# Grouped instance normalisation on one core: normalising on VectorE alone with half the instructions, and two early loads on the ScalarE queue

## Chip, core and metric

The kernel runs on one core of a Trainium2 chip. The metric is the device time of one execution in microseconds (us). The span that a profile shows is about 1.7 us shorter than that time. Where two kernels are compared by a ratio, it is the mean time of one kernel's fast runs over the mean of the other's of the same rounds, so it is not quite the ratio of the medians that are quoted.

## The reference

Shortened:

```python
def setup_inputs():
    B, G, C_per_g, H, W = 4, 8, 16, 256, 256       # x: 512 channels of 65536 float32, gamma: 128
    ...

def reference(x, gamma):
    mu = x.mean(axis=(3, 4), keepdims=True)
    var = ((x - mu) ** 2).mean(axis=(3, 4), keepdims=True)
    x_norm = (x - mu) / np.sqrt(var + 1e-5)
    return (x_norm * gamma[None, :, :, None, None]).astype(np.float32)
```

134.22 MB come in and 134.22 MB go out; every element is read once and written once.

## The kernel before

The input is cut into 32 units of 16 channels. A unit is a tile of 128 partitions by 8192 columns, 4 MB: a channel lies on 8 partitions. The kernel keeps six tiles in the on-chip memory. A unit is loaded, its sums and sums of squares are taken per partition, a small matmul averages them over the 8 partitions of a channel (its result, the tile `ps`, lies in the memory that the program calls PSUM), a row of tiny operations makes a scale and a shift, VectorE normalises 5376 columns and ScalarE the other 2816, and the unit is stored. Loads go out on the SyncE queue, stores on the ScalarE queue. Load u+6 waits until store u has freed its tile (26 waits of the SyncE queue for stores in the trace, 502.8 us in all).

```python
    for u in range(6):
        load(u)                                     # all on nc.sync
    g_row = singles.tile([1, G * C], F32, name="g_row")
    nc.scalar.dma_start(out=g_row[:], in_=gv[None, :])
    # ... constants, the averaging matrix, gamma brought to one value per partition ...

    def coefficients(u):
        # ... sums: one reduce_sum over 8192 columns; sqs: two Square activations of 4096 columns ...
        mv = stats_pool.tile([P, 2], F32, name="mv")
        nc.vector.reduce_sum(out=mv[:, 0:1], in_=sums[:], axis=AX.X)
        nc.vector.reduce_sum(out=mv[:, 1:2], in_=sqs[:], axis=AX.X)
        # ... matmul with avg into ps ...
        nc.vector.tensor_copy(out=cm[:], in_=ps[:])
        # ... nmean = -mean; var = E[x^2] - mean^2; std (ScalarE Sqrt); rstd; scale = rstd * gamma ...
        nc.vector.tensor_mul(out=shift[:], in0=nmean[:], in1=scale[:])
        return scale, shift
    # ...
    for u in range(U):
        scale, shift = coefficients(u)
        t = tiles.pop(u)
        # ... (store_spans is empty)
            norm_vector(t, 0, DV, scale, shift)     # DV = 5376
            norm_scalar(t, DV, F, scale, shift)
            nc.scalar.dma_start(out=ov[u], in_=t[:])
        if u + 6 < U:
            load(u + 6)
```

Of the kernel before, what the change touches and what calls it, by code (L numbers as in the profile page):

```python
# [6 lines left out]

F32 = mybir.dt.float32
BF16 = mybir.dt.bfloat16
ALU = mybir.AluOpType  # L10
ACTF = mybir.ActivationFunctionType
AX = mybir.AxisListType


@with_exitstack
def kernel(
    ctx: ExitStack,
    tc: tile.TileContext,
    x: bass.AP,
    gamma: bass.AP,  # L20
    out: bass.AP,
):
    nc = tc.nc
    B, G, C, H, W = x.shape
    P = nc.NUM_PARTITIONS
    HW = H * W
    n_ch = B * G * C
    S = 8
    K = P // S
    F = HW // S  # L30
    U = n_ch // K
    NG = (G * C) // K
    SQ = 4096
    DV = 5376
    assert HW % S == 0 and (G * C) % K == 0 and F % SQ == 0

    xv = x.rearrange("b g c h w -> (b g c h w)").rearrange("(u p f) -> u p f", p=P, f=F)
    ov = out.rearrange("b g c h w -> (b g c h w)").rearrange("(u p f) -> u p f", p=P, f=F)
    gv = gamma.rearrange("g c -> (g c)")

    data = ctx.enter_context(tc.tile_pool(name="data", bufs=6))
    singles = ctx.enter_context(tc.tile_pool(name="singles", bufs=1))
    stats_pool = ctx.enter_context(tc.tile_pool(name="stats", bufs=2))
    psum = ctx.enter_context(tc.tile_pool(name="psum", bufs=2, space=bass.MemoryType.PSUM))
    ctx.enter_context(tc.manual_schedule())

    def spans(widths):
        edges = [0]
        for w in widths:
            edges.append(edges[-1] + w)  # L50
        assert edges[-1] == F
        return list(zip(edges[:-1], edges[1:]))

    load_spans, store_spans = {}, {}
    whole = spans([F])

    tiles = {}

    def load(u):
        t = data.tile([P, F], F32, name="xt")  # L60
        for a, b in load_spans.get(u, whole):
            nc.sync.dma_start(out=t[:, a:b], in_=xv[u, :, a:b])
        tiles[u] = t

    for u in range(6):
        load(u)


    g_row = singles.tile([1, G * C], F32, name="g_row")
    nc.scalar.dma_start(out=g_row[:], in_=gv[None, :])  # L70
    eps_t = singles.tile([P, 1], F32, name="eps_t")
    nc.vector.memset(eps_t[:], 1e-5)
    avg = singles.tile([P, K, S], F32, name="avg")
    nc.gpsimd.memset(avg[:], 1.0 / HW)
    nc.gpsimd.affine_select(
        out=avg[:], in_=avg[:], pattern=[[-S, K], [0, S]], compare_op=ALU.is_ge,
        fill=0.0, base=0, channel_multiplier=1,
    )
    nc.gpsimd.affine_select(
        out=avg[:], in_=avg[:], pattern=[[S, K], [0, S]], compare_op=ALU.is_ge,  # L80
        fill=0.0, base=S - 1, channel_multiplier=-1,
    )
    one = singles.tile([1, 1], F32, name="one")
    nc.vector.memset(one[:], 1.0)
    g_rep = singles.tile([1, NG, K, S], F32, name="g_rep")
    nc.vector.tensor_copy(  # L86
        out=g_rep[:],
        in_=g_row[:].rearrange("o (n k) -> o n k", n=NG).unsqueeze(3).to_broadcast([1, NG, K, S]),
    )
    g_ps = psum.tile([P, NG], F32, name="g_ps", bufs=1)  # L90
    for n in range(NG):
        nc.tensor.matmul(  # L92
            out=g_ps[:, n : n + 1],
            lhsT=g_rep[:, n].rearrange("o k s -> o (k s)"),
            rhs=one[:],
            start=True, stop=True,
        )
    g_col = singles.tile([P, NG], F32, name="g_col")
    nc.vector.tensor_copy(out=g_col[:], in_=g_ps[:])  # L99

    junk = singles.tile([P, SQ], BF16, name="junk")

    def coefficients(u):
        t = tiles[u]
        sums = stats_pool.tile([P, len(load_spans.get(u, whole))], F32, name="sums")
        sqs = stats_pool.tile([P, F // SQ], F32, name="sqs")
        n = 0
        for j, (a, b) in enumerate(load_spans.get(u, whole)):
            nc.vector.reduce_sum(out=sums[:, j : j + 1], in_=t[:, a:b], axis=AX.X)  # L109
            for c in range(a, b, SQ):  # L110
                nc.scalar.activation(  # L111
                    out=junk[:], in_=t[:, c : c + SQ], func=ACTF.Square,
                    accum_out=sqs[:, n : n + 1],
                )
                n += 1
        mv = stats_pool.tile([P, 2], F32, name="mv")
        nc.vector.reduce_sum(out=mv[:, 0:1], in_=sums[:], axis=AX.X)  # L117
        nc.vector.reduce_sum(out=mv[:, 1:2], in_=sqs[:], axis=AX.X)  # L118
        ps = psum.tile([P, 2], F32, name="ps")
        nc.tensor.matmul(  # L120
            out=ps[:], lhsT=avg[:].rearrange("p k s -> p (k s)"), rhs=mv[:],
            start=True, stop=True,
        )
        cm = stats_pool.tile([P, 2], F32, name="cm")
        nc.vector.tensor_copy(out=cm[:], in_=ps[:])  # L125
        nmean = stats_pool.tile([P, 1], F32, name="nmean")
        nc.vector.tensor_scalar(  # L127
            out=nmean[:], in0=cm[:, 0:1], scalar1=-1.0, scalar2=None, op0=ALU.mult,
        )
        var = stats_pool.tile([P, 1], F32, name="var")  # L130
        nc.vector.scalar_tensor_tensor(  # L131
            out=var[:], in0=cm[:, 0:1], scalar=nmean[:], in1=cm[:, 1:2],
            op0=ALU.mult, op1=ALU.add,
        )
        std = stats_pool.tile([P, 1], F32, name="std")
        nc.scalar.activation(out=std[:], in_=var[:], func=ACTF.Sqrt, bias=eps_t[:], scale=1.0)  # L136
        rstd = stats_pool.tile([P, 1], F32, name="rstd")
        nc.vector.reciprocal(out=rstd[:], in_=std[:])  # L138
        scale = stats_pool.tile([P, 1], F32, name="scale")
        g = u % NG  # L140
        nc.vector.tensor_mul(out=scale[:], in0=rstd[:], in1=g_col[:, g : g + 1])  # L141
        shift = stats_pool.tile([P, 1], F32, name="shift")
        nc.vector.tensor_mul(out=shift[:], in0=nmean[:], in1=scale[:])  # L143
        return scale, shift

    def norm_vector(t, a, b, scale, shift):
        nc.vector.tensor_scalar(  # L147
            out=t[:, a:b], in0=t[:, a:b], scalar1=scale[:], scalar2=shift[:],
            op0=ALU.mult, op1=ALU.add,
        )  # L150

    def norm_scalar(t, a, b, scale, shift):
        nc.scalar.activation(  # L153
            out=t[:, a:b], in_=t[:, a:b], func=ACTF.Identity, bias=shift[:], scale=scale[:],
        )

    for u in range(U):
        scale, shift = coefficients(u)
        t = tiles.pop(u)
        if u in store_spans:  # L160
            for j, (a, b) in enumerate(store_spans[u]):
                (norm_scalar if j == 1 else norm_vector)(t, a, b, scale, shift)
            for a, b in store_spans[u]:
                nc.scalar.dma_start(out=ov[u, :, a:b], in_=t[:, a:b])
        else:
            norm_vector(t, 0, DV, scale, shift)
            norm_scalar(t, DV, F, scale, shift)
            nc.scalar.dma_start(out=ov[u], in_=t[:])
        if u + 6 < U:
            load(u + 6)  # L170


# [28 lines left out]
```

## Time and profile before

| | before |
|---|---|
| time, median of 3 runs | 628.93 us (628.9 to 629.06) |
| span of the profile | 627.1 us |
| instructions | 937, of them 324 on VectorE and 194 on ScalarE |
| bytes moved | 268.4 MB, mean 428 GB/s |
| VectorE / ScalarE busy | 66% / 54% |

The first lines come from the page of the kernel before: the span, busy time by engine (PE is TensorE and PEld its weight loads, DVE is VectorE, ACT is ScalarE, POOL is GpSimd), two rows of 40 slices of 15.7 us each (busy tenths of the 16 DMA engines, and GB/s), and the DMA queues. Queue q1 carries the loads, q10 the stores and the gamma row; q14 is the one whose kind the page gives as `instruction`.

```profile
span 627.1 us, 937 instructions
...
PE 22.3 (4%) x80; PEld 19.5 (3%) x80; DVE 416.5 (66%) x324; ACT 336.9 (54%) x194; POOL 1.2 (0%) x7
...
DMA  8999999999999999999999999999999999999997
GB/s 368 435 403 433 435 435 435 433 435 435 435 433 435 435 435 431 433 428 433 435 427 435 431 435 433 433 433 435 435 433 435 435 435 435 433 433 435 435 433 314
...
q1 hardware_dynamic: 4608, 134.22, 49.9%
q10 hardware_dynamic: 4610, 134.22, 49.6%
q14 instruction: 6, 0.05, 0.0%
```

The DMA engines are busy nine tenths or more in every slice but the first and the last, at 427 to 435 GB/s in all of these but the third (403). At 433 GB/s, the rate of the trace from 50 to 620 us, the bytes alone need 620 us, so the kernel stands within 1.5% of the time that its traffic takes at that rate. No compute engine is near its limit: the busiest, VectorE, works 66% of the span.

The next lines are the costliest groups of instructions (busy us, mean ns of one, then the engine's idle time before them and what ended it).

```profile
L109 DVE TENSOR_REDUCE sums<-xt 128x1 f32<-128x8192 f32 x32 | 277.9, 8686 | 150.4 <-DMA xt<-in_x_dram 150.4
L111 ACT ACTIVATE junk<-xt 128x4096 bf16<-128x4096 f32 x64 | 231.5, 3617 | 166.8 <-DMA xt<-in_x_dram 163.5
L147 DVE TENSOR_SCALAR xt<-xt,scale,shift 128x5376 f32<-128x5376 f32 x32 | 98.5, 3079 | 1.2
L153 ACT ACTIVATE xt<-xt,shift,scale 128x2816 f32<-128x2816 f32 x32 | 87.5, 2734 | 22.0 <-DVE shift L143 22.0
```

VectorE waits 150 us in all for loads. A unit's chain takes 14.2 us (from a reduction's start to the end of the normalise), and a unit lands every 19.35 us.

The last lines are of the view by windows: for stretches near the end, their length, each engine's busy time, the granted clock, the mean share of the 16 DMA engines that was busy, and GB/s.

```profile
core 0: us, PE busy (x) PEld busy (x) DVE busy (x) ACT busy (x) POOL busy (x), PEclk, DMA share, GB/s
...
620.00:622.00 2.00, 0.00 (x0) 0.00 (x0) 0.00 (x0) 0.00 (x0) 0.00 (x0) 1.00 0.68 295
622.00:624.00 2.00, 0.00 (x0) 0.00 (x0) 0.00 (x0) 0.00 (x0) 0.00 (x0) 1.00 0.65 279
624.00:626.00 2.00, 0.00 (x0) 0.00 (x0) 0.00 (x0) 0.00 (x0) 0.00 (x0) 1.00 0.08 33
626.00:628.00 2.00, 0.00 (x0) 0.00 (x0) 0.00 (x0) 0.00 (x0) 0.00 (x0) 1.00 0.00 0
```

A share of 0.06 would be one DMA engine of sixteen at work all the time; single windows read too high or too low where packets cross their edges (1.22 from 618 to 620 us, 0.68 from 620 to 622). Between 622 and 626 us the rate falls to 279 and then 33 GB/s.

The trace also has a record of every DMA packet. Each transfer of 4 MB gives every DMA engine eight packets of 32 KB, 1.213 us each (96% of them in this trace), and then a packet of 4 bytes, which I take for its report that it is done: each transfer has 128 of the large packets and 16 of these, and each of these starts within 0.013 us of the end of a data packet. So for the last store one can read when each engine finished (us after the first data packet, which comes 1.8 us into the span; lists of packets are on this clock, windows on the span's):

```
before, the 16 engines at the end of the last store:
621.53 621.54 621.55 621.58 621.59 621.60 621.62 621.68 621.69 621.71 621.71 621.72 621.76 622.56 623.45 623.93
```

Thirteen engines finish within 0.23 us, three come after, the last 2.24 us behind the median. The kernel ends with the last one: in all eleven profiles the span ends 1.3 to 1.6 us after it.

### The profile page before, as it was taken

How to read it: one execution, taken by the hardware profiler on the slowest of the kernel's cores; microseconds unless marked ns; L12 is line 12 of the kernel's file. 1: busy time of each engine (PE TensorE's matmuls, PEld its weight loads, DVE VectorE, ACT ScalarE, POOL GpSimd, SP SyncE). 2: the span in 40 equal slices, each digit the busy share in tenths (PEclk: the TensorE clock that was granted, in tenths of full speed). 3: DMA queues.
4: the chain of work that ended last, by engine and by line, in shares of the span. 5: the costliest groups of instructions: out<-in, count | busy, mean ns of one | idle time of the engine just before them, and what ended most of it. 6: DMA issues, size and time to landing. Idle time of an engine off the chain costs nothing.

```text
span 627.1 us, 937 instructions
## 1 busy us (share of the span) xinstructions
PE 22.3 (4%) x80; PEld 19.5 (3%) x80; DVE 416.5 (66%) x324; ACT 336.9 (54%) x194; POOL 1.2 (0%) x7
## 2 busy tenths in 40 slices
PE   2000000000000000000000000000000000000000
PEld 2000000000000000000000000000000000000000
DVE  2999657766577665686656866558665577655770
ACT  2877536555456464464634646446554455544560
POOL 0000000000000000000000000000000000000000
DMA  8999999999999999999999999999999999999997
GB/s 368 435 403 433 435 435 435 433 435 435 435 433 435 435 435 431 433 428 433 435 427 435 431 435 433 433 433 435 435 433 435 435 435 435 433 433 435 435 433 314
DMA packets 9224, 268.49 MB, mean 428 GB/s; under 512 B 1025, under 2 KB 1026, under 8 KB 1026
## 3 DMA queue, kind: packets, MB, share of 16 engines
q1 hardware_dynamic: 4608, 134.22, 49.9%
q10 hardware_dynamic: 4610, 134.22, 49.6%
q14 instruction: 6, 0.05, 0.0%
HBM read 134.22 MB, written 134.22 MB: 428 GB/s over the span
## 4 chain that ended last, share of the span: by engine, by line
DVE 67%; another core or an unknown queue 23%; PE 3%; DMA 2%; ACT 2%; issue 1%
DVE sums L109 44%; DVE xt L147 16%; PE ps L120 3%; DMA xt<-in_x_dram 2%; ACT std L136 2%; DVE var L131 1%; DVE rstd L138 1%; DVE cm L125 1%; DVE shift L143 1%; DVE scale L141 1%; DVE nmean L127 1%; DVE mv L117 1%; DVE mv L118 0%
## 5 line engine op out<-in xcount | busy, mean ns | idle before, releaser
L109 DVE TENSOR_REDUCE sums<-xt 128x1 f32<-128x8192 f32 x32 | 277.9, 8686 | 150.4 <-DMA xt<-in_x_dram 150.4
L111 ACT ACTIVATE junk<-xt 128x4096 bf16<-128x4096 f32 x64 | 231.5, 3617 | 166.8 <-DMA xt<-in_x_dram 163.5
L147 DVE TENSOR_SCALAR xt<-xt,scale,shift 128x5376 f32<-128x5376 f32 x32 | 98.5, 3079 | 1.2
L153 ACT ACTIVATE xt<-xt,shift,scale 128x2816 f32<-128x2816 f32 x32 | 87.5, 2734 | 22.0 <-DVE shift L143 22.0
L136 ACT ACTIVATE std<-var,eps_t 128x1 f32<-128x1 f32 x32 | 9.4, 294 | 85.4 <-DVE var L131 85.4
L120 PE MATMUL ps<-mv,avg 128*128 128x2 f32 x64 | 18.7, 362 | 582.9 <-DVE mv L118 582.9
L120 PEld LDWEIGHTS ps<-mv,avg 128*128 128x128 f32 x64 | 16.0, 311 | 585.6 <-DVE mv L118 569.8
L125 DVE COPY cm<-ps 128x2 f32<-128x2 f32 x32 | 5.1, 160 | 21.8 <-PE ps L120 21.8
L138 DVE RECIPROCAL rstd<-std 128x1 f32<-128x1 f32 x32 | 5.2, 164 | 11.6 <-ACT std L136 11.6
L111 ACT ACTIVATION_READ_ACCUMULATOR junk<-xt 128x1 f32 x64 | 11.9, 186 | 0.0
L131 DVE SCALAR_TENSOR_TENSOR var<-cm,nmean 128x1 f32<-128x1 f32 x32 | 7.0, 220 | 1.1
L143 DVE TENSOR_TENSOR shift<-nmean,scale 128x1 f32<-128x1 f32 x32 | 5.1, 159 | 1.1
L141 DVE TENSOR_TENSOR scale<-rstd,g_col 128x1 f32<-128x1 f32 x32 | 5.1, 159 | 1.1
L117 DVE TENSOR_REDUCE mv<-sums 128x1 f32<-128x1 f32 x32 | 4.9, 154 | 1.1
L127 DVE TENSOR_SCALAR nmean<-cm 128x1 f32<-128x1 f32 x32 | 4.9, 153 | 1.1
L118 DVE TENSOR_REDUCE mv<-sqs 128x1 f32<-128x2 f32 x32 | 4.7, 145 | 0.0
L92 PE MATMUL g_ps<-one,g_rep 1*128 1x1 f32 x16 | 3.6, 348 | 2.8 <-DVE g_rep L86 2.8
L92 PEld LDWEIGHTS g_ps<-one,g_rep 1*128 1x128 f32 x16 | 3.5, 325 | 2.8 <-DVE g_rep L86 2.8
L99 DVE COPY g_col<-g_ps 128x8 f32<-128x8 f32 x1 | 0.2, 167 | 3.7 <-PE g_ps L92 3.7
L111 ACT ACT_TABLE_LOAD x1 | 1.3, 1283 | 1.4 <-PEq L185 1.4
L86 DVE COPY g_rep<-g_row 1x1024 f32<-1x1024 f32 x1 | 0.7, 681 | 1.1 <-DMA g_row<-in_gamma_dram 1.1
L136 ACT ACT_TABLE_LOAD x1 | 1.3, 1283 | 0.0
(9 smaller groups left out, 1.5 us busy)
## 6 DMA issues: line engine op xcount, KB each, us to landing
xt<-in_x_dram SPq DMA_DIRECT2D x32, 4096.0 KB, 60.4
out_dram<-xt ACTq DMA_DIRECT2D x32, 4096.0 KB, 41.3
g_row<-in_gamma_dram ACTq DMA_DIRECT2D x1, 0.5 KB
```

What stands on the lines that cost most here:

```text
L109: nc.vector.reduce_sum(out=sums[:, j : j + 1], in_=t[:, a:b], axis=AX.X)
L111: nc.scalar.activation(out=junk[:], in_=t[:, c : c + SQ], func=ACTF.Square, accum_out=sqs[:, n : n + 1],)
L117: nc.vector.reduce_sum(out=mv[:, 0:1], in_=sums[:], axis=AX.X)
L120: nc.tensor.matmul(out=ps[:], lhsT=avg[:].rearrange("p k s -> p (k s)"), rhs=mv[:], start=True, stop=True,)
L125: nc.vector.tensor_copy(out=cm[:], in_=ps[:])
L131: nc.vector.scalar_tensor_tensor(out=var[:], in0=cm[:, 0:1], scalar=nmean[:], in1=cm[:, 1:2], op0=ALU.mult, op1=ALU.add,)
L136: nc.scalar.activation(out=std[:], in_=var[:], func=ACTF.Sqrt, bias=eps_t[:], scale=1.0)
L138: nc.vector.reciprocal(out=rstd[:], in_=std[:])
L141: nc.vector.tensor_mul(out=scale[:], in0=rstd[:], in1=g_col[:, g : g + 1])
L143: nc.vector.tensor_mul(out=shift[:], in0=nmean[:], in1=scale[:])
L147: nc.vector.tensor_scalar(out=t[:, a:b], in0=t[:, a:b], scalar1=scale[:], scalar2=shift[:], op0=ALU.mult, op1=ALU.add,)
L153: nc.scalar.activation(out=t[:, a:b], in_=t[:, a:b], func=ACTF.Identity, bias=shift[:], scale=scale[:],)
```

## The change

The intent was to drop work that the engines need not do: VectorE normalises the whole unit, the coefficients take fewer operations (the matmul gives minus the mean and minus the mean square, read straight from PSUM), one square of 8192 columns replaces two of 4096 (its unused output as uint8), tiles are fixed slots. Loads 1 and 3 go on the ScalarE queue, which has no stores yet. The core of the diff, shortened, with comments of mine:

```diff
-    for u in range(6):
-        load(u)
+    for u in range(AHEAD):                          # AHEAD = 6
+        load(u, nc.scalar if u in (1, 3) else nc.sync)
+        if u == 1:
+            nc.sync.dma_start(out=g_row[:], in_=gv[None, :])
 ... the averaging matrix holds -1/HW in place of 1/HW; gamma's columns are made within unit 0 ...
-            nc.vector.reduce_sum(out=sums[:, j : j + 1], in_=t[:, a:b], axis=AX.X)
-            for c in range(a, b, SQ):
-                nc.scalar.activation(out=junk[:], in_=t[:, c : c + SQ], func=ACTF.Square, accum_out=sqs[:, n : n + 1])
-        nc.vector.reduce_sum(out=mv[:, 0:1], in_=sums[:], axis=AX.X)
-        nc.vector.reduce_sum(out=mv[:, 1:2], in_=sqs[:], axis=AX.X)
-        nc.vector.tensor_copy(out=cm[:], in_=ps[:])
 ... nmean, var, shift ...
+        nc.vector.reduce_sum(out=st[:, u, 0:1], in_=t[:], axis=AX.X)
+        square = nc.scalar.activation(out=junk[:], in_=t[:], func=ACTF.Square, accum_out=st[:, u, 1:2])
+        nc.vector.tensor_scalar(                    # minus the variance
+            out=nvar[:, u : u + 1], in0=ps[:, 0:1], scalar1=ps[:, 0:1],
+            scalar2=ps[:, 1:2], op0=ALU.mult, op1=ALU.add)
 ... square root on ScalarE, reciprocal and product with gamma on VectorE, as before ...
-            norm_vector(t, 0, DV, scale, shift)
-            norm_scalar(t, DV, F, scale, shift)
+        nc.vector.tensor_scalar(
+            out=t[:], in0=t[:], scalar1=ps[:, 0:1], scalar2=scale[:, u : u + 1],
+            op0=ALU.add, op1=ALU.mult)
```

VectorE goes from 10 instructions a unit to 5, ScalarE from 6 to 3.

More of the change, by code (lines that the diff above doesn't have):

```diff
@@ L8 @@
 F32 = mybir.dt.float32
-BF16 = mybir.dt.bfloat16
+U8 = mybir.dt.uint8
 ALU = mybir.AluOpType
@@ L32 @@
     NG = (G * C) // K
-    SQ = 4096
-    DV = 5376
-    assert HW % S == 0 and (G * C) % K == 0 and F % SQ == 0
+    AHEAD = 6
+    assert HW % S == 0 and (G * C) % K == 0
     xv = x.rearrange("b g c h w -> (b g c h w)").rearrange("(u p f) -> u p f", p=P, f=F)
@@ L39, with load @@
     gv = gamma.rearrange("g c -> (g c)")
-    data = ctx.enter_context(tc.tile_pool(name="data", bufs=6))
+    data = ctx.enter_context(tc.tile_pool(name="data", bufs=1))
     singles = ctx.enter_context(tc.tile_pool(name="singles", bufs=1))
-    stats_pool = ctx.enter_context(tc.tile_pool(name="stats", bufs=2))
-    psum = ctx.enter_context(tc.tile_pool(name="psum", bufs=2, space=bass.MemoryType.PSUM))
+    psum = ctx.enter_context(tc.tile_pool(name="psum", bufs=4, space=bass.MemoryType.PSUM))
     ctx.enter_context(tc.manual_schedule())
-    def spans(widths):
-        edges = [0]
-        for w in widths:
-            edges.append(edges[-1] + w)
-        assert edges[-1] == F
-        return list(zip(edges[:-1], edges[1:]))
-    load_spans, store_spans = {}, {}
-    whole = spans([F])
-    tiles = {}
-    def load(u):
-        t = data.tile([P, F], F32, name="xt")
-        for a, b in load_spans.get(u, whole):
-            nc.sync.dma_start(out=t[:, a:b], in_=xv[u, :, a:b])
-        tiles[u] = t
-    for u in range(6):
-        load(u)
+    slots = [data.tile([P, F], F32, name=f"xt{i}") for i in range(AHEAD)]
+    def load(u, queue):
+        queue.dma_start(out=slots[u % AHEAD][:], in_=xv[u])
     g_row = singles.tile([1, G * C], F32, name="g_row")
-    nc.scalar.dma_start(out=g_row[:], in_=gv[None, :])
+    for u in range(AHEAD):
+        load(u, nc.scalar if u in (1, 3) else nc.sync)
+        if u == 1:
+            nc.sync.dma_start(out=g_row[:], in_=gv[None, :])
     eps_t = singles.tile([P, 1], F32, name="eps_t")
-    nc.vector.memset(eps_t[:], 1e-5)
-    avg = singles.tile([P, K, S], F32, name="avg")
-    nc.gpsimd.memset(avg[:], 1.0 / HW)
+    nc.gpsimd.memset(eps_t[:], 1e-5)
+    one = singles.tile([1, 1], F32, name="one")
+    nc.gpsimd.memset(one[:], 1.0)
+    navg = singles.tile([P, K, S], F32, name="navg")
+    nc.gpsimd.memset(navg[:], -1.0 / HW)
     nc.gpsimd.affine_select(
-        out=avg[:], in_=avg[:], pattern=[[-S, K], [0, S]], compare_op=ALU.is_ge,
+        out=navg[:], in_=navg[:], pattern=[[-S, K], [0, S]], compare_op=ALU.is_ge,
         fill=0.0, base=0, channel_multiplier=1,
@@ L79 @@
     nc.gpsimd.affine_select(
-        out=avg[:], in_=avg[:], pattern=[[S, K], [0, S]], compare_op=ALU.is_ge,
+        out=navg[:], in_=navg[:], pattern=[[S, K], [0, S]], compare_op=ALU.is_ge,
         fill=0.0, base=S - 1, channel_multiplier=-1,
     )
-    one = singles.tile([1, 1], F32, name="one")
-    nc.vector.memset(one[:], 1.0)
+    navg_w = navg[:].rearrange("p k s -> p (k s)")
     g_rep = singles.tile([1, NG, K, S], F32, name="g_rep")
-    nc.vector.tensor_copy(
-        out=g_rep[:],
-        in_=g_row[:].rearrange("o (n k) -> o n k", n=NG).unsqueeze(3).to_broadcast([1, NG, K, S]),
-    )
@@ L90 @@
     g_ps = psum.tile([P, NG], F32, name="g_ps", bufs=1)
-    for n in range(NG):
-        nc.tensor.matmul(
-            out=g_ps[:, n : n + 1],
-            lhsT=g_rep[:, n].rearrange("o k s -> o (k s)"),
-            rhs=one[:],
-            start=True, stop=True,
-        )
-    g_col = singles.tile([P, NG], F32, name="g_col")
-    nc.vector.tensor_copy(out=g_col[:], in_=g_ps[:])
-    junk = singles.tile([P, SQ], BF16, name="junk")
-    def coefficients(u):
-        t = tiles[u]
-        sums = stats_pool.tile([P, len(load_spans.get(u, whole))], F32, name="sums")
-        sqs = stats_pool.tile([P, F // SQ], F32, name="sqs")
-        n = 0
-        for j, (a, b) in enumerate(load_spans.get(u, whole)):
-            nc.vector.reduce_sum(out=sums[:, j : j + 1], in_=t[:, a:b], axis=AX.X)
-            for c in range(a, b, SQ):
-                nc.scalar.activation(
-                    out=junk[:], in_=t[:, c : c + SQ], func=ACTF.Square,
-                    accum_out=sqs[:, n : n + 1],
-                )
-                n += 1
-        mv = stats_pool.tile([P, 2], F32, name="mv")
-        nc.vector.reduce_sum(out=mv[:, 0:1], in_=sums[:], axis=AX.X)
-        nc.vector.reduce_sum(out=mv[:, 1:2], in_=sqs[:], axis=AX.X)
@@ new lines, with gamma_columns @@
+    g_col = singles.tile([P, NG], F32, name="g_col")
+    def gamma_columns():
+        nc.vector.tensor_copy(
+            out=g_rep[:],
+            in_=g_row[:].rearrange("o (n k) -> o n k", n=NG).unsqueeze(3).to_broadcast([1, NG, K, S]),
+        )
+        for n in range(NG):
+            nc.tensor.matmul(
+                out=g_ps[:, n : n + 1],
+                lhsT=g_rep[:, n].rearrange("o k s -> o (k s)"),
+                rhs=one[:],
+                start=True, stop=True,
+            )
+        nc.vector.tensor_copy(out=g_col[:], in_=g_ps[:])
@@ new lines @@
+    junk = singles.tile([P, F], U8, name="junk")
+    st = singles.tile([P, U, 2], F32, name="st")
+    nvar = singles.tile([P, U], F32, name="nvar")
+    std = singles.tile([P, U], F32, name="std")
+    rstd = singles.tile([P, U], F32, name="rstd")
+    scale = singles.tile([P, U], F32, name="scale")
+    squares = []
+    for u in range(U):
+        t = slots[u % AHEAD]
+        nc.vector.reduce_sum(out=st[:, u, 0:1], in_=t[:], axis=AX.X)
+        square = nc.scalar.activation(
+            out=junk[:], in_=t[:], func=ACTF.Square, accum_out=st[:, u, 1:2],
+        )
+        if u:
+            tc.declare_no_dep(square.ins, squares[-1].ins, reason="junk, ordered by the root between")
+        squares.append(square)
+        if u == 0:
+            gamma_columns()
@@ L119, in coefficients @@
         ps = psum.tile([P, 2], F32, name="ps")
-        nc.tensor.matmul(
-            out=ps[:], lhsT=avg[:].rearrange("p k s -> p (k s)"), rhs=mv[:],
-            start=True, stop=True,
-        )
-        cm = stats_pool.tile([P, 2], F32, name="cm")
-        nc.vector.tensor_copy(out=cm[:], in_=ps[:])
-        nmean = stats_pool.tile([P, 1], F32, name="nmean")
+        nc.tensor.matmul(out=ps[:], lhsT=navg_w, rhs=st[:, u], start=True, stop=True)
+        nc.vector.tensor_scalar(
+            out=nvar[:, u : u + 1], in0=ps[:, 0:1], scalar1=ps[:, 0:1],
+            scalar2=ps[:, 1:2], op0=ALU.mult, op1=ALU.add,
+        )
@@ L127, in coefficients @@
+        nc.scalar.activation(
+            out=std[:, u : u + 1], in_=nvar[:, u : u + 1], func=ACTF.Sqrt,
+            bias=eps_t[:], scale=-1.0,
+        )
+        nc.vector.reciprocal(out=rstd[:, u : u + 1], in_=std[:, u : u + 1])
+        g = u % NG
+        nc.vector.tensor_mul(
+            out=scale[:, u : u + 1], in0=rstd[:, u : u + 1], in1=g_col[:, g : g + 1],
+        )
         nc.vector.tensor_scalar(
-            out=nmean[:], in0=cm[:, 0:1], scalar1=-1.0, scalar2=None, op0=ALU.mult,
-        )
@@ L130, in coefficients @@
-        var = stats_pool.tile([P, 1], F32, name="var")
-        nc.vector.scalar_tensor_tensor(
-            out=var[:], in0=cm[:, 0:1], scalar=nmean[:], in1=cm[:, 1:2],
-            op0=ALU.mult, op1=ALU.add,
-        )
-        std = stats_pool.tile([P, 1], F32, name="std")
-        nc.scalar.activation(out=std[:], in_=var[:], func=ACTF.Sqrt, bias=eps_t[:], scale=1.0)
-        rstd = stats_pool.tile([P, 1], F32, name="rstd")
-        nc.vector.reciprocal(out=rstd[:], in_=std[:])
-        scale = stats_pool.tile([P, 1], F32, name="scale")
@@ L140, in coefficients @@
-        g = u % NG
-        nc.vector.tensor_mul(out=scale[:], in0=rstd[:], in1=g_col[:, g : g + 1])
-        shift = stats_pool.tile([P, 1], F32, name="shift")
-        nc.vector.tensor_mul(out=shift[:], in0=nmean[:], in1=scale[:])
-        return scale, shift
-    def norm_vector(t, a, b, scale, shift):
-        nc.vector.tensor_scalar(
-            out=t[:, a:b], in0=t[:, a:b], scalar1=scale[:], scalar2=shift[:],
-            op0=ALU.mult, op1=ALU.add,
-        )
-    def norm_scalar(t, a, b, scale, shift):
-        nc.scalar.activation(
-            out=t[:, a:b], in_=t[:, a:b], func=ACTF.Identity, bias=shift[:], scale=scale[:],
-        )
@@ L157 @@
-    for u in range(U):
-        scale, shift = coefficients(u)
-        t = tiles.pop(u)
-        if u in store_spans:
-            for j, (a, b) in enumerate(store_spans[u]):
-                (norm_scalar if j == 1 else norm_vector)(t, a, b, scale, shift)
-            for a, b in store_spans[u]:
-                nc.scalar.dma_start(out=ov[u, :, a:b], in_=t[:, a:b])
-        else:
-            norm_vector(t, 0, DV, scale, shift)
-            norm_scalar(t, DV, F, scale, shift)
-            nc.scalar.dma_start(out=ov[u], in_=t[:])
-        if u + 6 < U:
-            load(u + 6)
+            out=t[:], in0=t[:], scalar1=ps[:, 0:1], scalar2=scale[:, u : u + 1],
@@ L174 @@
+            op0=ALU.add, op1=ALU.mult,
+        )
+        nc.scalar.dma_start(out=ov[u], in_=t[:])
+        if u + AHEAD < U:
+            load(u + AHEAD, nc.sync)
 _INS = ['x', 'gamma']
```

## The prediction

> **What bounds the kernel now.** The DMA engines. The kernel moves 134.22 MB in and 134.22 MB out. The DMA row of the page shows nine tenths or more in all but the first and last of the 40 slices, and the GB/s row 427 to 435 in nearly all. [...] At 433 the 268.4 MB need 620 us; the span is 627.1. So about 7 us can be won: the start (1.2 us) and ramp, a dip where the first store begins (262 GB/s in the stretch 30 to 32 us, about 1 us lost), and a tail (314 GB/s in the last slice: the last bytes land near 625 us, then about 2 us of completion).
> No compute engine binds: DVE is busy 66%, ACT 54%. Once a unit has landed its chain takes 14.2 us (reduction 8.69, ten small steps near 2.5, normalise 3.08) and the next lands 19.3 us after it; the waits give DVE 150 us for loads. The chain of waits names DVE at 67%; that is not a bound.
>
> **What the change does, per unit.**
> - ACT's normalise, 2.73 us, goes. DVE does all 8192 columns: 3078 ns for 5376[...] scales to 4.5 to 4.7 us (estimate), so +1.5 us on DVE.
> - Two small reductions, the copy out of PSUM, the negation and the shift go: about 0.8 to 1.0 us of chain.
> - Two squares of 3.62 us become one of about 7.1 us (estimate), behind the reduction.
> Chain 14.2 -> about 14.8 us, still under 19.3. DVE about 455 us busy.
> - Scalar 1 is now in PSUM. [...] This trace doesn't test it. If lost, the normalise is about 8.7 us, the chain 19 us, DVE the bound, and the time near 645 to 650.
>
> **Queues.** Before, loads run alone for 27.5 us (2.75 units) and then share evenly with stores; the loads end at 598 us, leaving about 26 us of stores alone. The last store is issued at 612.8, about a microsecond before the one ahead of it is through: almost no slack. After, units 0 and 1 share the rate and land together near 21 us (unit 0 landed at 13.0), 2 and 3 near 40. Unit 0's chain also takes in the gamma columns (+5 us), so store 0 is ready near 41 us, as its queue comes free. The loads then lead by about 4 units in place of 2.75, loads end near 580, the last store is issued near 596 to 598 and waits behind two others. DMA stays full.
>
> **Sum.** Bytes and rate unchanged. Critical path: perhaps -1 us (the dip at the first store goes or moves, tail slack), perhaps +1 (two reading streams at the start).
>
> Predicted: 628.0 us, range 626.0 to 630.5; faster by over 2% 0.01, within 2% 0.93, slower by over 2% 0.06.
>
> **Right if** the GB/s row stays at 433 to 435, units 0 and 1 land together near 21 us, the last load lands near 580, the full-width normalise takes 4.5 to 4.7 us, and DVE waits for loads. **Wrong if** the normalise takes over 8 us, either queue runs dry with the other idle, or both loads together read slower than 433.

The time before, 628.93 us when it was made, with -1 and +1 comes to 628.9 us; the point is 628.0. The +1 for two reading streams is a guess that no trace stood behind. The 4.5 to 4.7 us of the normalise is an estimate that scales 3.08 us for 5376 columns (4.69 us in proportion). That this rate would stay was the expectation, and "if lost" is its loss: the 8.7 us are then an estimate from the reduction, 8.69 us for 8192 columns.

## The result, and the profile after

| | before | after |
|---|---|---|
| time, median of 4 runs | 628.99 us (628.9 to 629.29) | 627.0 us (626.8 to 627.19) |
| ratio of the fast runs, 95% interval | | 0.9967 (0.995 to 0.9985) |
| span | 627.1 us | 625.1 us |
| instructions | 937 | 628 |
| packets on the instruction queue within the span | 6 | 2 |
| last store: median engine / last engine | 621.69 / 623.93 | 621.12 / 621.80 |

By the 2% measure the two are the same; but every run after was shorter than every run before, by about 2 us. The page after:

```profile
span 625.1 us, 628 instructions
...
PE 21.4 (3%) x80; PEld 19.5 (3%) x80; DVE 442.9 (71%) x162; ACT 239.9 (38%) x98; POOL 1.3 (0%) x9
...
DMA  8999999999999999999999999999999999999998
GB/s 371 434 436 419 419 436 436 436 436 436 435 436 435 428 426 436 426 436 436 434 436 436 434 434 432 428 432 426 436 436 434 436 436 434 434 436 428 428 436 359
...
q10 hardware_dynamic: 4896, 142.61, 52.8%
q1 hardware_dynamic: 4322, 125.83, 46.8%
q14 instruction: 2, 0.02, 0.0%
```

The rate in the middle is what it was. The last slice moves 359 GB/s in place of 314, and q14 has 2 packets in place of 6. The groups:

```profile
L102 DVE TENSOR_REDUCE st<-xt 128x1 f32<-128x8192 f32 x32 | 277.9, 8684 | 110.2 <-DMA xt<-in_x_dram 110.2
L103 ACT ACTIVATE junk<-xt 128x8192 uint8<-128x8192 f32 x32 | 224.9, 7030 | 266.1 <-DMA xt<-in_x_dram 212.1
L127 DVE TENSOR_SCALAR xt<-xt,ps,scale 128x8192 f32<-128x8192 f32 x32 | 145.6, 4550 | 1.2
```

The normalise of all 8192 columns takes 4.55 us, within the predicted 4.5 to 4.7. ScalarE is 97 us less busy, VectorE 26 us more, and VectorE still waits 110 us for loads. The same windows near the end:

```profile
core 0: us, PE busy (x) PEld busy (x) DVE busy (x) ACT busy (x) POOL busy (x), PEclk, DMA share, GB/s
...
620.00:622.00 2.00, 0.00 (x0) 0.00 (x0) 0.00 (x0) 0.00 (x0) 0.00 (x0) 1.00 1.10 475
622.00:624.00 2.00, 0.00 (x0) 0.00 (x0) 0.00 (x0) 0.00 (x0) 0.00 (x0) 1.00 0.12 49
624.00:626.00 2.00, 0.00 (x0) 0.00 (x0) 0.00 (x0) 0.00 (x0) 0.00 (x0) 1.00 0.03 8
626.00:628.00 2.00, 0.00 (x0) 0.00 (x0) 0.00 (x0) 0.00 (x0) 0.00 (x0) 1.00 0.00 0
```

```
after, the 16 engines at the end of the last store:
620.91 620.92 620.93 620.93 620.94 621.05 621.07 621.11 621.13 621.18 621.19 621.23 621.24 621.46 621.62 621.80
```

The 8 GB/s in the window from 624 to 626 us are one packet of 16 KB on yet another queue, after the kernel's own transfers. I call the distance from the median engine to the last the lag of the slowest engine. The finishing times split the gain. The last engine ends 2.13 us earlier; the median engine accounts for 0.57 us of it, and 1.56 us is the lag of the slowest engine, 0.68 us in place of 2.24.

Where does the lag come from? Taken at the end of each store, it does not grow evenly but in steps, and each step falls on a packet of the instruction queue (I call such a packet a fetch):

```
lag of the slowest engine behind the median, us (first column: us after the first data packet, end of a store)
before, instruction packets at 76.8 115.6 319.7 398.1 503.8 552.9
   69: 0.25    89: 0.67   ...  302: 0.54   322: 1.42   ...  496: 1.43   535: 1.54   555: 2.27   ...  624: 2.24
after, instruction packets at 159.9 196.2
  142: 0.23   162: 0.73   ...  297: 0.68   ...  622: 0.68
```

The steps come after the packets at 76.8, 319.7 and 552.9 us, 243 and 233 us or 12 to 12.5 units apart. Between them the trace has 140 and 132 VectorE instructions (10 a unit, and one in most units that only waits), and the packets are 8192 bytes. The other three leave the slowest engine's lag almost as it is; followed packet by packet they lie on other engines of the sixteen, where the data packets behind them take 1.46, 1.47 and 1.63 us in place of 1.213. One such packet in the records of the kernel before (start, end and length in us, queue, bytes), with the data packets of the same DMA engine around it:

```
318.446  319.659  1.213   q10  32768
319.655  319.964  0.309   q14   8192
319.961  321.755  1.794   q1   32768
```

The instruction packet holds the engine for 0.31 us, and the data packet behind it takes 0.58 us longer than its 1.213. So one fetch costs this engine 0.89 us. Nothing gives that back (the lag stays at 1.43 us from 341 to 496 us): from 50 to 620 us the mean busy share of the sixteen engines is 1.00, so none has idle time to catch up in, and each engine carries an equal share, 512 of the 8192 large packets.

### The profile page after: what moved, and what is told of

It reads as the page before. It is cut to its first block, busy times and chain, and to the rows that moved or that the text cites. A ratio compares the mean times of both kernels' runs of the same rounds, so it can differ in the third digit from the quotient of the medians.

```text
span 625.1 us, 628 instructions
## 1 busy us (share of the span) xinstructions
PE 21.4 (3%) x80; PEld 19.5 (3%) x80; DVE 442.9 (71%) x162; ACT 239.9 (38%) x98; POOL 1.3 (0%) x9
## 4 chain that ended last, share of the span: by engine, by line
DMA 62%; DVE 30%; PE 2%; issue 1%; ACT 1%; SPq 0%; ACTq 0%
DMA xt<-in_x_dram 55%; DVE st L102 24%; DMA out_dram<-xt 7%; DVE xt L127 5%; PE ps L113 2%; DVE nvar L114 1%; PE g_ps L83 1%; ACT std L118 0%; ACT L118 0%; DVE rstd L122 0%; DVE scale L124 0%; DVE g_rep L78 0%; SPq L48 0%; ACTq L118 0%
## 5 line engine op out<-in xcount | busy, mean ns | idle before, releaser
L102 DVE TENSOR_REDUCE st<-xt 128x1 f32<-128x8192 f32 x32 | 277.9, 8684 | 110.2 <-DMA xt<-in_x_dram 110.2
L103 ACT ACTIVATE junk<-xt 128x8192 uint8<-128x8192 f32 x32 | 224.9, 7030 | 266.1 <-DMA xt<-in_x_dram 212.1
L127 DVE TENSOR_SCALAR xt<-xt,ps,scale 128x8192 f32<-128x8192 f32 x32 | 145.6, 4550 | 1.2
L118 ACT ACTIVATE std<-nvar,eps_t 128x1 f32<-128x1 f32 x32 | 9.4, 295 | 76.0 <-DVE nvar L114 76.0
L113 PE MATMUL ps<-st,navg 128*128 128x2 f32 x64 | 17.9, 349 | 536.4 <-DVE st L102 536.4
L113 PEld LDWEIGHTS ps<-st,navg 128*128 128x128 f32 x64 | 16.0, 311 | 538.2 <-issue 538.2
L114 DVE TENSOR_SCALAR nvar<-ps 128x1 f32<-128x1 f32 x32 | 9.2, 286 | 23.4 <-PE ps L113 23.4
L103 ACT ACTIVATION_READ_ACCUMULATOR junk<-xt 128x1 f32 x32 | 6.0, 186 | 0.0
```

What stands on the lines that cost most here:

```text
L102: nc.vector.reduce_sum(out=st[:, u, 0:1], in_=t[:], axis=AX.X)
L103: square = nc.scalar.activation(out=junk[:], in_=t[:], func=ACTF.Square, accum_out=st[:, u, 1:2],)
L113: nc.tensor.matmul(out=ps[:], lhsT=navg_w, rhs=st[:, u], start=True, stop=True)
L114: nc.vector.tensor_scalar(out=nvar[:, u : u + 1], in0=ps[:, 0:1], scalar1=ps[:, 0:1], scalar2=ps[:, 1:2], op0=ALU.mult, op1=ALU.add,)
L118: nc.scalar.activation(out=std[:, u : u + 1], in_=nvar[:, u : u + 1], func=ACTF.Sqrt, bias=eps_t[:], scale=-1.0,)
L127: nc.vector.tensor_scalar(out=t[:], in0=t[:], scalar1=ps[:, 0:1], scalar2=scale[:, u : u + 1], op0=ALU.add, op1=ALU.mult,)
```

## The experiments

Theory F: the gain comes from fewer instruction fetches, which delay one DMA engine of a kernel that is bound by all sixteen. Theory Q, the rival that the prediction had leaned on: the gain comes from the order of loads and stores on the queues (a smaller dip at the first store, a fuller tail). A second rival, C: it comes from the compute change itself, VectorE alone normalising. All of these kernels gave correct results. They ran in three groups; within each the kernel before ran beside them, at 628.93, 628.9 and 628.9 us. In the first group one of its nine runs took 631.04 us, counted as fast, which is why I go by medians.

### The queue part undone

```diff
-        load(u, nc.scalar if u in (1, 3) else nc.sync)
+        load(u, nc.sync)
         if u == 1:
-            nc.sync.dma_start(out=g_row[:], in_=gv[None, :])
+            nc.scalar.dma_start(out=g_row[:], in_=gv[None, :])
```

> The changed kernel with all six first loads on the SyncE queue again (the queue part undone); instructions and mid-run instruction fetches as in the changed kernel (2). Theory F (the 2 us come from the slowest DMA engine, which each mid-run instruction fetch of 8 KB holds up by about 0.9 us; 6 fetches before, 2 after): stays at 627.0 to 627.6 us. Theory Q (the 2 us come from the order of loads and stores on the two queues: fuller tail, smaller dip at the first store): back to 628.6 to 629.2.

Measured: 627.03 us (626.98 to 627.13, 5 runs; ratio 0.9966, 0.9952 to 0.998), 2 fetches, lag 0.75 us. All of the gain is there without the queue part. The dip is even back at its old place (407 GB/s in the third slice of 40, as in the kernel before with 403). Q falls as an account of the gain. With two loads on the other queue the time was 627.0 us, without 627.03.

### The queue part alone

```diff
-            nc.sync.dma_start(out=t[:, a:b], in_=xv[u, :, a:b])
+            (nc.scalar if u in (1, 3) else nc.sync).dma_start(out=t[:, a:b], in_=xv[u, :, a:b])
```
(in the kernel before, with the gamma row issued ahead of the loads)

> The kernel before with loads 1 and 3 moved to the ScalarE queue ahead of the stores (the queue part alone); 6 fetches as before. F: 628.3 to 629.1 us. Q: 626.8 to 627.3.

Measured: 628.62 us (628.42 to 629.04); ratio to the kernel before 0.9992 (0.9979 to 1.0004), so not told apart from it. The profile, taken in the slowest of the five runs, has 6 fetches: the median engine ends at 621.11, earlier than before's 621.69, but the slowest at 624.18, a lag of 3.08 us. The queue part may help all engines by half a microsecond; the lag hides it.

### Five tiny VectorE instructions a unit put back

```diff
+        for _ in range(5):
+            nc.vector.memset(fill[:], 0.0)          # 128 x 1, nothing reads it
         ps = psum.tile([P, 2], F32, name="ps")
```

> The changed kernel with 5 one-element memsets a unit added on VectorE (160 in all, about 0.3 us of chain a unit, VectorE still idle for over 2 us a unit), so VectorE's instruction count is back at about 322 and its fetches at 3. F: 627.8 to 628.8 us, 4 mid-run fetches, the spread of the DMA engines' last packets up from 0.9 to about 2 us. Q, or a theory that says compute work off the path costs nothing whatever its instruction count: 626.8 to 627.2.

Measured: 628.83 us (628.76 to 629.26), 4 fetches at 99.8, 196.4, 313.6 and 555.3 us. From its page:

```profile
q14 instruction: 4, 0.03, 0.0%
...
L104 DVE TENSOR_REDUCE st<-xt 128x1 f32<-128x8192 f32 x32 | 277.9, 8684 | 112.3 <-DMA xt<-in_x_dram 112.3
L115 DVE MEMSET fill<- 128x1 f32 x160 | 9.4, 59 | 8.9
```

VectorE still waits 112 us for loads, as much as without the memsets (110), so it is not their 9.4 us of work that the time shows. The lag steps from 0.14 to 0.90, from 0.82 to 1.67 and from 1.67 to 2.56 us after the first, third and last. The two runs above say what the gain is not; this one gives nearly all of it back with 160 instructions that compute nothing. The upper end of the expectation was 628.8, so the median is just over it; the spread of the engines' last packets rose from 0.9 to 2.9 us, where about 2 was expected.

### Thirteen a unit

The same edit with `range(13)`.

> The changed kernel with 13 one-element memsets a unit on VectorE (416 in all, some 1 us of chain a unit, VectorE still idle). Fetch theory: 5 VectorE fetches in place of 1, each 0.85 to 0.9 us on one DMA engine, the slowest DMA engine 4.5 us behind the rest: 630.0 to 631.0 us, slower than the kernel before. Theory that only engine work on the path counts: 626.8 to 627.3.

Measured: 630.59 us (630.39 to 631.02), ratio 1.0028 (1.0015 to 1.004): slower than the kernel before. Six fetches in all, as before, but five on VectorE's stream: the lag steps after each of these, and not after the one at 203.7 us. VectorE still waits 91 us for loads. The windows near its end:

```profile
core 0: us, PE busy (x) PEld busy (x) DVE busy (x) ACT busy (x) POOL busy (x), PEclk, DMA share, GB/s
...
622.00:624.00 2.00, 0.00 (x0) 0.00 (x0) 0.00 (x0) 0.00 (x0) 0.00 (x0) 1.00 0.35 147
624.00:626.00 2.00, 0.00 (x0) 0.00 (x0) 0.00 (x0) 0.00 (x0) 0.00 (x0) 1.00 0.04 16
626.00:628.00 2.00, 0.00 (x0) 0.00 (x0) 0.00 (x0) 0.00 (x0) 0.00 (x0) 1.00 0.04 16
```

A share of 0.04 in 2 us is a single packet of 1.2 us. By the packet records fifteen engines are done at 622.07 at the latest, and one works on to 625.52 (627.3 us of the span), a lag of 4.11 us or 0.82 us a fetch. So the total count does not decide: before had six as well. What counts is how many fall on one DMA engine. The later VectorE fetches come 136.4 us apart (302.2, 438.6, 575.1), 7.05 units at 18 VectorE instructions each, 127 instructions to a fetch of 8192 bytes.

### 1280 tiny GpSimd instructions

```diff
+    for _ in range(1280):
+        nc.gpsimd.memset(fill[:], 0.0)              # 1 x 1, nothing reads it
```
(ahead of the loop over units)

> The changed kernel with 1280 one-element memsets on GpSimd, which nothing waits for. F: about 9 to 10 more fetches of 8 KB in the trace, all on GpSimd's instruction stream; if one DMA engine serves it, that engine lags 8 to 9 us and the time is 633 to 636 us; if they spread over the engines, 627 to 629. Q: 626.8 to 627.3, no change.

Measured: 632.39 us (632.35 to 632.67), ratio 1.0052 (1.0039 to 1.0065). Ten fetches more, as expected; a smaller cost than expected, 633 having been the low end. The lag is 6.16 us, about 0.6 us for each of the ten, because the data packets behind these fetches took 0.2 to 0.35 us longer and not, as behind most VectorE fetches, 0.53 to 0.63. The ten fetches and what the packets behind them took longer add up to 6.0 us. (At the ends of stores the lag is 4.95 us up to 573 us and 6.16 from 589, one packet's time more as the loads end, with no fetch between; I have no run on that last step.) The 1280 instructions bring ten fetches of 8192 bytes, so an instruction has 64 bytes by estimate (81920 over 1280). Two places of the profile show it, the queue lines and the windows near the end:

```profile
q14 instruction: 12, 0.10, 0.0%
```

```profile
core 0: us, PE busy (x) PEld busy (x) DVE busy (x) ACT busy (x) POOL busy (x), PEclk, DMA share, GB/s
...
622.00:624.00 2.00, 0.00 (x0) 0.00 (x0) 0.00 (x0) 0.00 (x0) 0.00 (x0) 1.00 0.27 115
624.00:626.00 2.00, 0.00 (x0) 0.00 (x0) 0.00 (x0) 0.00 (x0) 0.00 (x0) 1.00 0.11 49
626.00:628.00 2.00, 0.00 (x0) 0.00 (x0) 0.00 (x0) 0.00 (x0) 0.00 (x0) 1.00 0.04 16
628.00:630.00 2.00, 0.00 (x0) 0.00 (x0) 0.00 (x0) 0.00 (x0) 0.00 (x0) 1.00 0.04 16
```

Again one engine works on alone, to 629.3 us of the span. VectorE's normalise took 4.55 us in this run too.

### The control: GpSimd busy with few instructions

```diff
+    for _ in range(110):
+        nc.gpsimd.memset(fill[:], 0.0)              # 128 x 512
```

> Control for the run with 1280 memsets: GpSimd busy for 70 us or more with 110 long memsets (128 x 512) in place of many short ones. Fetch theory: 0 or 1 fetch more than the changed kernel, 626.8 to 627.6 us. Rival, that GpSimd's being busy[...] slowed the kernel in the earlier run: 628.5 or more.

Measured: 627.3 us (627.2 to 627.49), 3 fetches, lag 0.80 us. GpSimd was busy 72 us here and 171 us in the run before it, so the doses are not equal; but 72 us of work with one fetch cost 0.3 us, and 171 us with ten cost 5.4.

### The kernel before with thinner statistics

```diff
-        nc.vector.reduce_sum(out=sums[:, j : j + 1], in_=t[:, a:b], axis=AX.X)     # and two squares of 4096
-        nc.vector.reduce_sum(out=mv[:, 0:1], in_=sums[:], axis=AX.X)
-        nc.vector.reduce_sum(out=mv[:, 1:2], in_=sqs[:], axis=AX.X)
+        nc.vector.reduce_sum(out=mv[:, 0:1], in_=t[:], axis=AX.X)
+        nc.scalar.activation(out=junk[:], in_=t[:], func=ACTF.Square, accum_out=mv[:, 1:2])
```
(shortened; junk becomes uint8 of 8192 columns)

> The kernel before with only its statistics thinned: one square of 8192 columns, both sums written straight into the pair that the matmul reads. VectorE 324 to 260 instructions, ScalarE 194 to 130; the split normalise, the one load queue and the rest as before. Fetch theory: 2 VectorE fetches in place of 3, 3 or 4 in all in place of 6, the slowest DMA engine 0.9 us less behind: 627.8 to 628.4 us. Theory that the gain is in the order of the queues, or in who normalises: 628.7 to 629.2.

Measured: 628.37 us (628.02 to 628.7), ratio 0.9992 (0.9978 to 1.0006). The median is where F put it, but the interval cannot tell it from no change. The profile does: the lag is 1.41 us in place of 2.24, with a step at 398.2 us (0.44 to 1.30). Five fetches in all, where F had counted on three or four.

### The normalise shared again

```diff
-            out=t[:], in0=t[:], scalar1=ps[:, 0:1], scalar2=scale[:, u : u + 1],
+            out=t[:, :5376], in0=t[:, :5376], scalar1=ps[:, 0:1], scalar2=scale[:, u : u + 1],
+        nc.scalar.activation(out=t[:, 5376:], in_=t[:, 5376:], func=ACTF.Identity,
+            bias=shift[:, u : u + 1], scale=scale[:, u : u + 1])
```
(in the changed kernel, with one VectorE product for the shift)

> The changed kernel with its normalise shared again, 5376 columns on VectorE and 2816 on ScalarE (one instruction more a unit on each). Fetch theory: 626.8 to 627.6 us, at most one fetch more on each engine. Theory that the gain comes from VectorE alone normalising: 628.5 or more.

Measured: 627.91 us (627.71 to 628.17), between the two expectations. I had put no price on the fetches that its extra instructions bring: 5 in place of 2, with lag steps at 122 us (0.27 to 1.10) and 537 us (1.04 to 1.87). The lag rises by 1.16 us over the changed kernel's, which is more than the 0.9 us of time. By these figures who normalises matters only through the instructions that it takes, and nothing is left for C.

### The lag against the fetches

| kernel | VectorE instructions | fetches, all | with a step of the lag | slowest engine's lag, us | time, us |
|---|---|---|---|---|---|
| changed | 162 | 2 | 1 | 0.68 | 627.0 |
| changed, one queue | 162 | 2 | 1 | 0.75 | 627.03 |
| changed, long memsets | 162 | 3 | 1 | 0.80 | 627.3 |
| changed, split normalise | 194 | 5 | 2 | 1.84 | 627.91 |
| before, thin statistics | 260 | 5 | 2 | 1.41 | 628.37 |
| before, two queues | 324 | 6 | 3 | 3.08 | 628.62 |
| changed, 5 fills | 322 | 4 | 3 | 2.56 | 628.83 |
| before | 324 | 6 | 3 | 2.24 | 628.99 |
| changed, 13 fills | 578 | 6 | 5 | 4.11 | 630.59 |
| changed, 1280 on GpSimd | 162 | 12 | 10 | 6.16 | 632.39 |

The fourth column counts the fetches on one stream, VectorE's or in the last row GpSimd's, that the slowest engine served; the lag goes with it and not with the count of all. (For GpSimd the early steps do not show singly, and the ten are those of its stream.) The times are medians of each kernel's own rounds; the lag is from one profiled run. Among variants of the changed kernel the time less the lag is 626.1 to 626.5 us. The kernel before and its two variants stray further, by up to 0.8 us; the median engine is not the same in all of them, and the 3.08 us of the one with two queues is from the slowest of its runs.

### A kernel that computes too slowly, on purpose

```diff
-        nc.vector.tensor_scalar(out=t[:], in0=t[:], scalar1=ps[:, 0:1], scalar2=scale[:, u : u + 1],
-            op0=ALU.add, op1=ALU.mult)
+        nc.vector.scalar_tensor_tensor(out=t[:], in0=t[:], scalar=ps[:, 0:1],
+            in1=scale[:, u : u + 1].to_broadcast([P, F]), op0=ALU.add, op1=ALU.mult)
```

> The changed kernel with the normalise written as a two-source operation (the scale broadcast as second source)[...]: 8.6 to 8.7 us in place of 4.55. VectorE then has about 19.0 us of work and waits a unit against the 19.35 us that the DMA gives it. If the step of the prediction holds that VectorE becomes the bound: loads land at 22.6 us, gamma columns about 7 us, 32 units of 19.0 us, a last store alone of 9.7 us and 2 us of completion make 645 to 650 us. If the lead that the kernel has in buffers absorbs it: under 632.

(That a form with two sources would take about the reduction's 8.68 us was the estimate.)

Measured: 654.4 us (654.34 to 654.47), ratio 1.0405 (1.0387 to 1.0422).

```profile
span 652.7 us, 628 instructions
...
PE 21.4 (3%) x80; PEld 19.5 (3%) x80; DVE 575.6 (88%) x162; ACT 239.9 (37%) x98; POOL 1.3 (0%) x9
...
DMA  9999999999999999999999999999999999994555
GB/s 386 420 448 400 432 430 436 432 436 432 436 426 440 426 440 426 442 426 442 424 444 424 442 424 442 426 440 428 438 428 438 430 434 434 432 434 203 225 257 257
...
L102 DVE TENSOR_REDUCE st<-xt 128x1 f32<-128x8192 f32 x32 | 277.7, 8678 | 22.6 <-DMA xt<-in_x_dram 22.6
L127 DVE SCALAR_TENSOR_TENSOR xt<-xt,ps,scale 128x8192 f32<-128x8192 f32 x32 | 280.2, 8756 | 1.1
```

The direction is right and the size too small. VectorE is now the bound: it waits for no load after the first, and its unit takes 19.13 us (583.01 to 602.14) where I had 19.0, 4 us over 32 units; and I summed a span and called it a time, which is 1.7 us. The run shows two more things. A unit of 19.13 us is under the 19.35 that the DMA gives, and still VectorE is the bound: it starts at 22.6 us, its last unit ends at 640.5, and the last store comes after that. So the changed kernel, with 15.05 us a unit, has less room than the difference of 4.3 us: the span of 652.7 is 27.6 us or 0.86 us a unit too long, so by estimate VectorE becomes the bound at about 18.3 us a unit. And in this run, where VectorE is the bound, two fetches leave a lag of 0.09 us: the DMA engines were busy only four to five tenths of the last four slices, at 203 to 257 GB/s, so the one behind had time to catch up.

## Why the prediction was right, and what it missed

The time, 627.0 us, lies in the range of 626.0 to 630.5 and 1.0 us under the point. The range is wide: the kernel before, at 628.93 us, lies in it too. That nothing large would change was argued and came out; that 2 us were won came from a term that the prediction did not have, and that the time still fell in the range is owed to its width, not to the sum: luck in that part.

- The bound was right. The DMA moved 429 GB/s on the mean after and 428 before, and 426 to 436 in all slices after but the ends and the dip (the prediction had said 433 to 435). From 50 to 620 us both traces have 433 GB/s at a busy share of 1.00.
- Of the engine work, the costs were right: normalise 4.55 us (said: 4.5 to 4.7), square 7.03 us (about 7.1), a unit's chain 15.05 us (about 14.8), VectorE busy 443 us (about 455). They are off the path, as said.
- The rate of the normalise held with a scalar in PSUM: 8192 columns in 4.55 us, 1.80 a ns, where the kernel before, with both its scalars in tiles outside PSUM, took 3.08 us for 5376, 1.75 a ns. The form with two sources took 8.76 us for 8192, 0.94 a ns. That the rate stays is what the trace shows.
- The queue picture was right in its times: units 0 and 1 land together at 22.6 us (near 21), the last unit lands at 580.4 us (near 580), the last store is issued at 595.5 us (596 to 598). Store 0 was ready at 43.1 us and not 41: unit 0 landed later than said, and its square root had to wait for a table load of 1.28 us.
- The step that failed is the sum's "perhaps -1 us (the dip at the first store goes or moves, tail slack)". The dip moved and did not go: 403 GB/s in the third slice before, 419 in the fourth and fifth after. And the queue part, to which this term belonged, is worth nothing that shows in the changed kernel (627.03 against 627.0 us) and 0.3 us by the medians in the old one (628.62 against 628.93), where the interval of the ratio reaches from a gain of 1.3 us to a loss of 0.3. What was gained came from a term that the sum does not have: instruction fetches on the DMA engines, 1.56 of 2.13 us.
- The prediction read the tail (314 GB/s in the last slice) as late stores and completion. Of the 3.6 us from the median engine's end to the span's end, 2.24 are the lag of the slowest of sixteen, late by the fetches that it had served, and 1.4 lie between its last packet and the span's end. "Tail slack" was not what was short: the kernel with one queue keeps the tail's order and has the gain.

The other 0.57 us, by which the median engine ends earlier, is not settled. Both kernels with one queue and the old normalise have it late (621.69 and 621.61), the changed kernel with one queue less so (621.33), those with two queues at 621.1 to 621.4. I have no run that says why. The fetches near 504 to 516 us, in the kernel before, its two variants and the split normalise, seem to be SyncE's: in all four traces 79 SyncE instructions stand before them (of 95 in all), and the kernels with 70 or 71 SyncE instructions have no such fetch.

I ran no version beyond the changed kernel that could beat it: what the lag still holds is 0.68 us, one fetch on VectorE's stream. Whether a cut of a few more instructions would spare that one was not tested.

## What to carry to other kernels

When a kernel is bound by its DMA engines, look at when each of the sixteen finishes, not only at the mean rate: here the slowest decided, 2.24 us behind the median engine before and 0.68 after, and with the engines' busy share at 1.00 it did not catch up (1.43 us from 341 to 496 us before, 0.68 from 297 to 622 us after). Instructions that look free because their engine idles are fetched by those same DMA engines, here at 0.5 to 0.9 us for most fetches of 8 KB; trimming tiny instructions from the engine whose fetches the slowest DMA engine serves (here VectorE) was worth that much each. And test a bundle's parts apart: here the part that looked like the reason for the gain did nothing that shows (627.03 us without it, 627.0 with it).
